# Seven Strassen units at the front of four up groups, with more room for their sums, in a one-layer hybrid decoder kernel

## The chip, the core and the metric

The kernel runs as one program on one core of a Trainium2 chip. The core's engines work from queues of their own and wait for each other by semaphores: PE multiplies matrices, DVE (VectorE) and ACT (ScalarE) do elementwise work, POOL (GpSimd) and SP issue DMAs. The metric is the device time of one execution, in microseconds (us); the time given is the median of several runs.

## What is computed

The reference computes one layer in float32 on 256 rows of 2048 channels:

```python
h = x
a = rmsnorm(h, attn_norm);  proj = a @ w_in          # two attentions follow, 16 heads
h = h + concat(out_mla, out_moba) @ w_o
f = rmsnorm(h, ffn_norm)
h = h + (silu(f @ w_gate) * (f @ w_up)) @ w_down     # w_gate, w_up: 2048 x 5632; w_down: 5632 x 2048
g = sigmoid(rmsnorm(h, ple_norm) @ w_ple_gate)
h = h + g * (p @ w_ple_proj);  out = rmsnorm(h, final_norm)
```

The change concerns the third part, the SwiGLU network, and there the four later products with w_up.

## The kernel before

**Three products for one.** A float32 product is made of float32r matmuls. Each operand is split into a high part, the operand rounded to float32r, and a low part, the rest. `three` (L350 to L352) issues the high activation by the high weight, the low activation by the high weight, and the high activation by the low weight. The high part of a weight is made by ACT (`split_hi`, L329, a CAST), the low part by DVE (`split_lo`, L337, raw minus high), which therefore waits for ACT.

**Groups, units, jobs.** A group is one product of the 256 rows with 1024 weight columns, accumulated in four PSUM banks (two row tiles by two column halves). It has units of two 128-row slices of the weight (1 MB of float32, one DMA into one of five raw buffers). A plain unit takes 2 slices x 2 halves x 2 row tiles x 3 = 24 matmuls of 128x512. The order of the groups in the SwiGLU network is g0, u0, then for c = 1 to 4: gate gc, the first half of the down product of the block before (dc0), up uc, the second half (dc1); then gu5 and the last down products. Gate and up groups have 8 units, down groups 4.

**Strassen units.** Some units of gate and up groups go by Strassen's scheme (in Winograd's form): the two slices by the two column halves are a 2x2 matrix of weight blocks, the two slices by the two row tiles one of activation blocks, and seven block products stand in for eight. `seven` (L392 on) issues them in four turns of 6, 3, 6 and 6 matmuls, 21 in all, into seven banks: three are the group's own, four others hold m1, m7, m5 and m6. In the run of such units of a group these four banks are taken from the rotating ones. After the last unit of the run ACT copies m1 to a tile U and DVE adds the other three in four instructions (L415 to L419). U is added to the group's banks when the group ends (L380 for an up group, by a DMA for a gate group).

The weights of such a unit cost more to prepare. `plan` gives it four jobs in place of two: the blocks "11 22" (1024 columns per partition), "21" (512), and the sums "t1 t3" and "t4 t2" (1024 each). Each job has a high part by ACT and a low part by DVE, and DVE makes the sums in three instructions (L340 with 1024 elements, L341 and L342 with 512), from raw, in place. A plain unit has two jobs of 1024. In down groups one job of 2048 does for the unit.

**The ring.** The parts lie in a ring of places of 512 columns: 12 in the ring proper, 4 in `more`, and 4 in `most`. A job takes 2 places (4 for a down unit's, 1 for "21"), and a job that would lie across the end of one of the three tiles begins at the next. `plan` notes for each job the last turn that reads the places it takes. The loop at the kernel's end puts a job's instructions in the queues of ACT and DVE ahead of turn j only if all turns that read its places are before j. So what ACT and DVE do is in the order of the jobs, and how far ahead of PE they are is bounded by the ring. Into the same queues go, at their place in the program, the evacuations: the four copies of a down group's banks at its end (`add_later`, L862, ACT, then a DMA by POOL that adds them to `hd` in DRAM), the silu (L969, ACT, two instructions, four steps after the gate group), the up group's end (L380 and L978, DVE), and the transposes of the block (`ff_transpose`: PE L1000, then ACT L121 and DVE L122, during the next gate group).

**Which units.** `mixed` names the eight units of a gate or up group in their order; S marks a Strassen unit. Before, the four later up groups and the gates from g2 on have '6 S0 S1 S2 S3 S4 S5 7': plain, six Strassen, plain. g0 has none, u0 two, g1 five.

**The activations' sums.** The scheme needs four sums of activation blocks per Strassen unit, split in high and low. `act_transpose` makes them when the activations are normed, during wo1 and g0 (L155 to L159). Before, three of the four get tiles of their own (`sums`, `sums4`, `sums5h`, `sums5l`); the fourth is kept in float32 (`s4`) and split later, by `fourth_sums`, into a quarter of aT that the plain units no longer read.

## Time and profile before

| | us |
|---|---|
| runs: median (lowest to highest) | 1192.59 (1191.95 to 1192.99), three runs |
| the profiled execution, span from first to last instruction | 1190.6 |
| PE busy with matmuls | 1179.3 (99%) |
| PE weight loads busy | 984.3 (83%) |
| DVE busy | 916.9 (77%) |
| ACT busy | 699.5 (59%) |
| POOL busy | 42.4 (4%) |

The profile gives no time of its execution beside the span; the span lies 2.0 us below the median of the runs. One period of the SwiGLU network (u, d1, next g, next d0) takes 124.8 us in it, and there are four. Times below are counted from the start of the span. Up group u2 begins on PE at 661.4, the down group d21 at 701.0, g3 at 722.7, d30 at 764.4 and u3 at 786.2. In a view in order of time, a row has the start in us, the duration in us, engine, line and operation, what is written from what, the count of merged instructions, and in brackets the idle time of the engine just before, with what ended it. PE rows last 0.39 us, but the matmuls overlap: the distance between two starts is what counts.

### The profile page before, as it was taken

What the parts mean: (1) busy time and instruction counts of PE and PEld (TensorE: products, weight loads), DVE (VectorE), ACT (ScalarE), POOL (GpSimd) and SP (SyncE); (2) the same over time, 40 slices, a digit from 0 to 9 for tenths busy, and PEclk for the clock granted to TensorE, in tenths of its full rate; (3) what the DMA queues carried; (4) which work ended last, traced back from release to release, by engine and by line L of the source; (5) the groups of instructions that cost most, each with busy time, mean ns of one, the idle gap of its engine ahead of it and who ended that gap; (6) DMA issues with size and microseconds to landing.
All of it is one profiled execution on the core that took longest, in us unless ns stands there. A gap on an engine that the chain in (4) does not pass through costs nothing.

```text
span 1190.6 us, 14471 instructions
## 1 busy us (share of the span) xinstructions
PE 1179.3 (99%) x5501; PEld 984.3 (83%) x5501; DVE 916.9 (77%) x1082; ACT 699.5 (59%) x898; POOL 42.4 (4%) x56
## 2 busy tenths in 40 slices
PE   9999999999999999999999999999999999999996
PEld 7888888899888888888888888888888888888886
DVE  5654635656457668998999899989998999897474
ACT  6735655456556755465656565757475656465453
POOL 5200000000000000000000000000000000000000
PEclk9999999999999999999999999999999999999998
DMA  9654654435653867395867777786869586836631
GB/s 305 213 190 122 214 168 151 150 111 199 247 210 112 315 222 273 107 308 167 297 182 258 231 240 225 221 274 207 252 217 276 193 256 212 339 138 219 210 106 71
DMA packets 79734, 250.30 MB, mean 210 GB/s; under 512 B 4844, under 2 KB 9248, under 8 KB 78384
## 3 DMA queue, kind: packets, MB, share of 16 engines
q1 hardware_dynamic: 75744, 229.93, 54.2%
q0 software_dynamic: 3632, 18.93, 8.8%
q8 instruction: 43, 0.70, 0.2%
q10 hardware_dynamic: 288, 0.52, 0.1%
q14 instruction: 27, 0.22, 0.1%
HBM read 228.39 MB, written 12.58 MB: 202 GB/s over the span
## 4 chain that ended last, share of the span: by engine, by line
PE 85%; DVE 9%; ACT 3%; issue 2%; DVEq 0%; ACTq 0%; POOL 0%; POOLq 0%
PE bank L352 27%; PE bank L350 27%; PE bank L351 27%; DVE ringl L337 3%; ACT ringh L329 1%; DVE raw L340 1%; PE bank L138 1%; DVE most L337 1%; PE bank L541 1%; DVE raw L341 1%; PE bank L662 1%; DVE raw L342 1%; PE bank L1000 1%; PE bank L570 0%; PE bank L544 0%
## 5 line engine op out<-in xcount | busy, mean ns | idle before, releaser
L337 DVE TENSOR_TENSOR ringl<-raw,ringh 128x1024 fp32r<-128x1024 f32 (+4 forms) x298 | 433.7, 1484 | 130.0 <-ACT ringh L329 124.1
L329 ACT CAST ringh<-raw 128x1024 fp32r<-128x1024 f32 (+4 forms) x298 | 366.0, 1263 | 283.7 <-PE bank L351 137.0
L350 PE MATMUL bank<-ringh,aT 128*128 128x512 f32 (+3 forms) x780 | 301.4, 386 | 0.0
L352 PE MATMUL bank<-ringl,aT 128*128 128x512 f32 (+3 forms) x780 | 296.8, 380 | 0.1
L351 PE MATMUL bank<-ringh,aT 128*128 128x512 f32 (+3 forms) x780 | 296.2, 380 | 0.0
L352 PEld LDWEIGHTS bank<-ringl,aT 128*128 128x128 f32 x780 | 146.5, 188 | 28.5 <-DVE ringl L337 1.5
L351 PEld LDWEIGHTS bank<-ringh,aT 128*128 128x128 f32 x780 | 146.8, 188 | 26.0
L350 PEld LDWEIGHTS bank<-ringh,aT 128*128 128x128 f32 x780 | 146.8, 188 | 26.0 <-ACT aT L124 0.3
L329 ACT CAST moreh<-raw 128x1024 fp32r<-128x1024 f32 (+2 forms) x68 | 79.1, 1192 | 45.2 <-DVE raw L340 36.0
L337 DVE TENSOR_TENSOR morel<-raw,moreh 128x1024 fp32r<-128x1024 f32 (+2 forms) x64 | 83.5, 1329 | 0.9 <-ACT moreh L329 0.2
L350 PE MATMUL bank<-ringh,ffTh 128*128 128x512 f32 x204 | 79.4, 389 | 0.0
L351 PE MATMUL bank<-ringh,ffTl 128*128 128x512 f32 x204 | 79.4, 389 | 0.0
L352 PE MATMUL bank<-ringl,ffTh 128*128 128x512 f32 x204 | 79.4, 389 | 0.0
L329 ACT CAST most<-raw 128x1024 fp32r<-128x1024 f32 (+2 forms) x55 | 54.6, 1017 | 35.9 <-DVE raw L340 30.6
L340 DVE TENSOR_TENSOR raw<-raw 128x1024 f32<-128x1024 f32 x57 | 69.5, 1219 | 0.0
L337 DVE TENSOR_TENSOR most<-raw,most 128x1024 fp32r<-128x1024 f32 (+2 forms) x55 | 63.2, 1171 | 1.8 <-ACT most L329 1.5
L352 PEld LDWEIGHTS bank<-ringl,ffTh 128*128 128x128 f32 x204 | 38.3, 188 | 8.0
L351 PEld LDWEIGHTS bank<-ringh,ffTl 128*128 128x128 f32 x204 | 38.3, 188 | 7.9
L350 PEld LDWEIGHTS bank<-ringh,ffTh 128*128 128x128 f32 x204 | 38.3, 188 | 7.9
L342 DVE TENSOR_TENSOR raw<-raw 128x512 f32<-128x512 f32 x57 | 39.5, 692 | 1.9
L341 DVE TENSOR_TENSOR raw<-raw 128x512 f32<-128x512 f32 x57 | 39.5, 692 | 1.9
L352 PE MATMUL bank<-most,aT 128*128 128x512 f32 x94 | 37.0, 394 | 0.0
(334 smaller groups left out, 1804.5 us busy)
## 6 DMA issues: line engine op xcount, KB each, us to landing
raw<-in_w_down SPq DMA_DIRECT2D x44, 1024.0 KB, 4.9
raw<-in_w_gate SPq DMA_DIRECT2D x40, 1024.0 KB, 7.0
raw<-in_w_up SPq DMA_DIRECT2D x40, 1024.0 KB, 8.3
raw<-in_w_in SPq DMA_DIRECT2D x40, 512.0 KB, 4.5
raw<-in_w_o SPq DMA_DIRECT2D x16, 1024.0 KB, 5.0
raw<-in_w_ple_gate SPq DMA_DIRECT2D x16, 1024.0 KB, 4.9
raw<-in_w_in SPq DMA_DIRECT2D x8, 1024.0 KB, 5.0
hd<-copied POOLq DMA_DIRECT2D x8, 1024.0 KB, 9.4
```

Of the source, the lines that this page charges most:

```text
L138: nc.tensor.transpose(b[:, (2 * i + t) * 128:(2 * i + t + 1) * 128], part[:, t, i * 128:(i + 1) * 128], ident)
L329: nc.scalar.copy(h[:, :, c0:c1], r[:, :, c0:c1])
L337: tt(l[:, :, c0:c1], r[:, :, c0:c1], h[:, :, c0:c1].bitcast(F32), op=ALU.subtract)
L340: tt(f[:, 0:2], f[:, 1:2].to_broadcast([128, 2, 512]), f[:, 0:4:3], op=ALU.subtract)
L341: tt(f[:, 3], f[:, 3], f[:, 0], op=ALU.subtract)
L342: tt(f[:, 2], f[:, 2], f[:, 3], op=ALU.subtract)
L350: nc.tensor.matmul(b, xh, h, start=start, stop=False)
L351: nc.tensor.matmul(b, xl, h, start=False, stop=False)
L352: nc.tensor.matmul(b, xh, l, start=False, stop=stop)
L541: nc.tensor.matmul(s[:, c0:c0 + nk], qT[:, q * 128:(q + 1) * 128], kT[:, 0:nk], start=True, stop=qpe is None)
L662: nc.tensor.transpose(b[:, (2 * i + t) * 128:(2 * i + t + 1) * 128], src[:, t, col(i0 + i):col(i0 + i) + 128], ident)
L1000: nc.tensor.transpose(b[:, (2 * i + t) * 128:(2 * i + t + 1) * 128], st[:, t, (k + i) * 128:(k + i + 1) * 128], ident)
```

## The change

1. `SEVENS` is 7 in place of 6, so that unit 6 has its activation sums too.
2. `mixed` gives the up groups u1 to u4 the order 'S0 S1 S2 S3 S4 S5 S6 7': seven Strassen units from the group's start, then one plain unit. The gate groups keep theirs.
3. All four sums of a unit are made and split at once in `act_transpose` (one split of 512 elements in place of 384), and `fourth_sums` with its calls is gone. The sums lie in `att`, a new tile `more_sums` (12 KB per partition), `tabs` and `ra`.
4. The room is taken from the scratch for the descriptors of DMAs that POOL issues: `dynamic_dma_scratch_size` is set to 4096 bytes per partition, where it was left at its default of 16384.
5. In `split_lo` the first sum of the weight blocks is issued ahead of the low part of "21" in place of behind it. This holds for all Strassen units. In the new numbering the low parts are L340 and the sums L339, L342 and L343.

```diff
@@ act_transpose
-        some = some.rearrange("q a (b c) -> q (a b) c", b=2)[:, 0:3]
+        four = some.rearrange("q a (b c) -> q (a b) c", b=2)
         tt = nc.vector.tensor_tensor
-        tt(some[:, 0], a21, a22, op=ALU.add)
-        tt(some[:, 1], some[:, 0], a11, op=ALU.subtract)
-        tt(some[:, 2], a21, a11, op=ALU.subtract)
-        tt(sums[2], a12, some[:, 1], op=ALU.subtract)
-        split_psum(sums[0], sums[1], some)
+        tt(four[:, 0], a21, a22, op=ALU.add)
+        tt(four[:, 2], a21, a11, op=ALU.subtract)
+        tt(four[:, 1], four[:, 0], a11, op=ALU.subtract)
+        tt(four[:, 3], a12, four[:, 1], op=ALU.subtract)
+        split_psum(sums[0], sums[1], four)
@@ split_lo
+        f = quarters(jb) if jb.kind == "21" else None
+        if f is not None:
+            tt(f[:, 0:2], f[:, 1:2].to_broadcast([128, 2, 512]), f[:, 0:4:3], op=ALU.subtract)
         tt(l[:, :, c0:c1], r[:, :, c0:c1], h[:, :, c0:c1].bitcast(F32), op=ALU.subtract)
-        if jb.kind == "21":
-            f = quarters(jb)
-            tt(f[:, 0:2], f[:, 1:2].to_broadcast([128, 2, 512]), f[:, 0:4:3], op=ALU.subtract)
+        if f is not None:
             tt(f[:, 3], f[:, 3], f[:, 0], op=ALU.subtract)
             tt(f[:, 2], f[:, 2], f[:, 3], op=ALU.subtract)
@@
-    SEVENS = 6
+    SEVENS = 7
@@ ffn_norm_half
-                    S["sums"] = big.tile([128, 2, 4, 3, 128], F32R, name="sums", tag="att")
...
+                    sums = [big.tile([128, 2, 3, 4, 128], F32R, name=f"sums{x}", tag=x) for x in ("att", "more_sums")]
+                    last = [big.tile([128, 4, 128], F32R, name="sums6h", tag="tabs"),
+                            work.tile([128, 4, 128], F32R, name="sums6l", tag="ra", bufs=1)]
+                    S["sums"] = [[x[:, i, n] for x in sums for n in range(3)] + [last[i]] for i in range(2)]
@@ gate_evac, gate_add, up_evac: the calls of fourth_sums go, and with them
-    def fourth_sums(*pairs):
-        for n in pairs:
-            split_psum(*(aT[i][:, 2 * n, 128:256] for i in range(2)), S["s4"][n])
@@ mixed
-        pairs = {'g0': '0 1 2 3 4 5 6 7', 'u0': '6 7 S0 S1 2 3 4 5', 'g1': '6 5 S0 S1 S2 S3 S4 7'}.get(name, '6 S0 S1 S2 S3 S4 S5 7').split()
+        pairs = {'g0': '0 1 2 3 4 5 6 7', 'u0': '6 7 S0 S1 2 3 4 5', 'g1': '6 5 S0 S1 S2 S3 S4 7'}.get(
+            name, '6 S0 S1 S2 S3 S4 S5 7' if name[0] == 'g' else 'S0 S1 S2 S3 S4 S5 S6 7').split()
@@
-    nc = bacc.Bacc("TRN2", target_bir_lowering=False, num_devices=1)
+    nc = bacc.Bacc("TRN2", target_bir_lowering=False, num_devices=1, dynamic_dma_scratch_size=4096)
```

What this does to the queues is shown at three places. In the rows, `raw_N` is the raw buffer of a unit, so the rows of one unit share it; ringh and ringl, moreh and morel, most are the high and low parts in the ring's three tiles.

**DVE, from the last unit of d20 to the front of u2.** Before: the job of d20's last unit (2048), unit 6 in two jobs, then S0 and the first of S1.

```order
L337 TENSOR_TENSOR ringl<-raw_113,ringh 128x2048
L337 TENSOR_TENSOR ringl<-raw_114,ringh 128x1024 x2
L337 TENSOR_TENSOR ringl<-raw_2796,ringh 128x1024
L337 TENSOR_TENSOR ringl<-raw_2796,ringh 128x512
L340 TENSOR_TENSOR raw_2796<-raw_2796 128x1024
L341 TENSOR_TENSOR raw_2796<-raw_2796 128x512
L342 TENSOR_TENSOR raw_2796<-raw_2796 128x512
L337 TENSOR_TENSOR morel<-raw_2796,moreh 128x1024 x2
L337 TENSOR_TENSOR most<-raw_2831,most 128x1024
L337 TENSOR_TENSOR most<-raw_2831,most 128x512
L340 TENSOR_TENSOR raw_2831<-raw_2831 128x1024
```

Now:

```order
L340 TENSOR_TENSOR morel<-raw_113,moreh 128x2048
L340 TENSOR_TENSOR most<-raw_114,most 128x1024
L339 TENSOR_TENSOR raw_114<-raw_114 128x1024
L340 TENSOR_TENSOR most<-raw_114,most 128x512
L342 TENSOR_TENSOR raw_114<-raw_114 128x512
L343 TENSOR_TENSOR raw_114<-raw_114 128x512
L340 TENSOR_TENSOR ringl<-raw_114,ringh 128x1024 x2
L340 TENSOR_TENSOR ringl<-raw_2796,ringh 128x1024
L339 TENSOR_TENSOR raw_2796<-raw_2796 128x1024
L340 TENSOR_TENSOR ringl<-raw_2796,ringh 128x512
L342 TENSOR_TENSOR raw_2796<-raw_2796 128x512
L343 TENSOR_TENSOR raw_2796<-raw_2796 128x512
```

S0 (raw_114) now follows d20's last unit directly, and S1 (raw_2796) follows S0; the first sum of a unit stands ahead of the low part of its "21".

**ACT, across the four copies at the end of d20** (L862 before, L863 now). Before:

```order
L329 CAST moreh<-raw_2796 128x1024 x2
L329 CAST most<-raw_2831 128x1024
L329 CAST most<-raw_2831 128x512
L862 COPY copied<-bank_77 128x512
L862 COPY copied<-bank_78 128x512
L862 COPY copied<-bank_79 128x512
L862 COPY copied<-bank_80 128x512
L329 CAST ringh<-raw_2831 128x1024 x2
L969 ACTIVATE stage<-stage,rf 128x1024 x2
L329 CAST ringh<-raw_112 128x1024
```

Now:

```order
L329 CAST ringh<-raw_2796 128x1024
L329 CAST ringh<-raw_2796 128x512
L329 CAST ringh<-raw_2796 128x1024 x2
L863 COPY copied<-bank_77 128x512
L863 COPY copied<-bank_78 128x512
L863 COPY copied<-bank_79 128x512
L863 COPY copied<-bank_80 128x512
L329 CAST moreh<-raw_2828 128x1024
L329 CAST moreh<-raw_2828 128x512
L951 ACTIVATE stage<-stage,rf 128x1024 x2
L329 CAST most<-raw_2828 128x1024 x2
```

Before, the copies stood within S1 (raw_2831), and the silu between S1 and S2. Now they stand between S1 (raw_2796) and S2 (raw_2828), and the silu within S2.

**DVE at the front of g3, around the four instructions on the transposed block** (L122). Before:

```order
L337 TENSOR_TENSOR ringl<-raw_113,ringh 128x1024
L337 TENSOR_TENSOR ringl<-raw_113,ringh 128x512
L340 TENSOR_TENSOR raw_113<-raw_113 128x1024
L341 TENSOR_TENSOR raw_113<-raw_113 128x512
L342 TENSOR_TENSOR raw_113<-raw_113 128x512
L337 TENSOR_TENSOR ringl<-raw_113,ringh 128x1024
L122 TENSOR_TENSOR ffTl<-bank_77,ffTh 128x512
L122 TENSOR_TENSOR ffTl<-bank_78,ffTh 128x512
L122 TENSOR_TENSOR ffTl<-bank_79,ffTh 128x512
L122 TENSOR_TENSOR ffTl<-bank_80,ffTh 128x512
L337 TENSOR_TENSOR morel<-raw_113,moreh 128x1024
L337 TENSOR_TENSOR morel<-raw_114,moreh 128x1024
```

Now:

```order
L340 TENSOR_TENSOR ringl<-raw_113,ringh 128x1024
L339 TENSOR_TENSOR raw_113<-raw_113 128x1024
L340 TENSOR_TENSOR ringl<-raw_113,ringh 128x512
L342 TENSOR_TENSOR raw_113<-raw_113 128x512
L343 TENSOR_TENSOR raw_113<-raw_113 128x512
L122 TENSOR_TENSOR ffTl<-bank_77,ffTh 128x512
L122 TENSOR_TENSOR ffTl<-bank_78,ffTh 128x512
L122 TENSOR_TENSOR ffTl<-bank_79,ffTh 128x512
L122 TENSOR_TENSOR ffTl<-bank_80,ffTh 128x512
L340 TENSOR_TENSOR ringl<-raw_113,ringh 128x1024 x2
L340 TENSOR_TENSOR morel<-raw_114,moreh 128x1024
```

The jobs lie at other places of the ring, and "t1 t3" of S1 (the sixth row before) has moved behind the transposed block, to its fellow "t4 t2". It is so in g2 and g3; in g4 and gu5 the order is as before.

More of the change, by code (lines that the diff above doesn't have):

```diff
@@ L900, in scale @@
                         nc.scalar.mul(S["nrm"][:, (k // 2) % 2, t], S["h"][:, t, k * 128:k * 128 + 256], S["rs"][:, t:t + 1])
-                if k0:
-                    s4 = work.tile([128, 2, 128], F32, name="s4c", tag="junk")
-                    S["s4"] += [s4[:, i] for i in range(2)]
-                    S["sums"][0].append(work.tile([128, 3, 128], F32R, name="sums5h", tag="ra", bufs=1))
-                    S["sums"][1].append(big.tile([128, 3, 128], F32R, name="sums5l", tag="mask"))
                 scale(k0)
@@ L912, in g @@
                 for k in range(k0, k0 + 8, 2):
-                    sums = [*(S["sums"][i][k // 2] for i in range(2)), S["s4"][k // 2]] if k // 2 < SEVENS else None
+                    sums = [S["sums"][i][k // 2] for i in range(2)] if k // 2 < SEVENS else None
                     act_transpose(S["h"], k, G_FFN, aT, scaled=True, sums=sums)
@@ L980, in f @@
             if left["n"] == 0:
-                if ci == 0:
-                    fourth_sums(*(2, 3, 4))
                 turned = ff_transpose(ci, n, S.pop("ff"))
```

11 lines of the change are left out of this document (removed).

## The prediction

> **What bounds the kernel now.** I read the page's busy times, then the busy times of one period of the SwiGLU network, then the chain of waits there, then PE and DVE in order of time.
>
> ```profile
> PE 1179.3 (99%) x5501; PEld 984.3 (83%) x5501; DVE 916.9 (77%) x1082; ACT 699.5 (59%) x898; POOL 42.4 (4%) x56
> ```
>
> ```profile
> 661.40:786.20 124.80, 124.75 (x558) 102.80 (x557) 117.24 (x119) 77.79 (x85) 3.92 (x4) 1.00 0.74 236
> ```
>
> Over the span PE looks like the only bound. In the period (second row: length, then busy PE, weight loads, DVE, ACT, POOL, granted clock) DVE is busy 117.24 of 124.8 us, 94%. The chain of waits of the same period runs more through DVE than through any line of PE:
>
> ```profile
> by line: DVE ringl L337 14.3%; PE bank L352 12.9%; PE bank L351 12.6%; PE bank L350 12.6%; issue 10.3%; DVE raw L340 7.3%; ACT ringh L329 5.7%; DVE raw L341 3.9%; DVE most L337 3.8%; DVE raw L342 3.1%; DVE U L380 1.9%; DVE stage L978 1.8%;
> ```
>
> Now PE in u2, first its front (start of the plain unit 6, start of S0), then the second half of its last unit's first bank, then a place in g3:
>
> ```profile
> 661.38 0.39 PE L350 MATMUL bank<-ringh,aT 128*128 128x512 f32 x1
> ...
> 666.82 0.39 PE L350 MATMUL bank<-ringh,aT 128*128 128x512 f32 x1
> ```
>
> ```profile
> 696.53 0.49 PE L352 MATMUL bank<-most,aT 128*128 128x512 f32 x1
> 696.87 0.40 PE L350 MATMUL bank<-moreh,aT 128*128 128x512 f32 x1
> ```
>
> ```profile
> 755.99 0.39 PE L351 MATMUL bank<-ringh,sums5l 128*128 128x512 f32 x1
> 756.43 0.50 PE L352 MATMUL bank<-ringl,sums5h 128*128 128x512 f32 x1
> ```
>
> 24 matmuls take 666.82 - 661.38 = 5.44 us, 0.227 each. A Strassen unit's 21 take 4.76. Two starts that lie further apart are a wait: 0.34 after the last low part of u2's weights (0.1 lost), and 0.44 within S5 of g3 (0.2 lost). Apart from steps of 0.1 where transposes stand between, these are the waits of the period, and both are for low parts (L352), that is for DVE. So PE never stops for long, but DVE is just in time at the end of both runs. Here is DVE from the last unit of d20 to the end of u2's jobs:
>
> ```profile
> 644.59 6.29 DVE L337 TENSOR_TENSOR ringl<-raw,ringh 128x2048 fp32r<-128x2048 f32 x5
> ...
> 656.37 1.83 DVE L337 TENSOR_TENSOR most<-raw,most 128x1024 fp32r<-128x1024 f32 x2 [0.49 <-ACT most L329]
> ...
> 663.15 2.36 DVE L337 TENSOR_TENSOR ringl<-raw,ringh 128x1024 fp32r<-128x1024 f32 x2 [2.37 <-ACT ringh L329]
> 667.12 1.83 DVE L337 TENSOR_TENSOR ringl<-raw,ringh 128x1024 fp32r<-128x1024 f32 x2 [1.61 <-ACT ringh L329]
> 668.87 1.22 DVE L340 TENSOR_TENSOR raw<-raw 128x1024 f32<-128x1024 f32 x1
> 670.12 0.69 DVE L341 TENSOR_TENSOR raw<-raw 128x512 f32<-128x512 f32 x1
> ...
> 675.61 1.22 DVE L340 TENSOR_TENSOR raw<-raw 128x1024 f32<-128x1024 f32 x1
> ...
> 695.26 1.22 DVE L337 TENSOR_TENSOR most<-raw,most 128x1024 fp32r<-128x1024 f32 x1
> 696.68 2.29 DVE L337 TENSOR_TENSOR ringl<-raw,ringh 128x2048 fp32r<-128x2048 f32 x1 [0.21 <-ACT ringh L329]
> ```
>
> From one unit's L340 to the next, 668.87 to 675.61, a Strassen unit takes DVE **6.74 us**, against 4.76 on PE. Within the run DVE falls behind by 2 us per unit and lives off its lead, which the ring bounds. From 667.12 (S2's first job) four units and the last unit's two jobs of 1.22 make 667.12 + 4 x 6.74 + 2.44 = 696.5; the last one does end at 695.26 + 1.22 = 696.48. So the run is DVE without a gap. DVE's idle time lies ahead of it: 0.49 + 2.37 + 1.61 = 4.47 us, all for ACT's high parts.
>
> **Part 1: fewer matmuls.** Four groups lose 3 matmuls each: 12 x 0.227 = 2.7 us of PE, 0.68 per group. This is a gain only where PE need not wait.
>
> **Part 2: DVE's work in an up group.** Unit 6 cost two jobs, 2.44 us; as a Strassen unit it costs 6.74: 4.30 us more per group. What of that fits into the 4.47 us of idle time is decided by the ring, at the group's front. I follow u2. DVE ends d20's last job at 644.59 + 2.29 = 646.9 (the first of the row's five; its length as in the row at 696.68) and has S0 and S1 ready 2 x 6.74 later, at 660.4. S2's first job takes places of the ring that d20's last unit holds (in all four groups); PE is done with that unit at 661.38, and ahead of S2's cast in ACT's queue now stand all four copies of d20's banks. The last copy waits for the same end of PE:
>
> ```profile
> 661.58 0.59 ACT L862 COPY copied<-bank 128x512 f32<-128x512 f32 x1 [0.77 <-PE bank L352]
> 662.07 2.00 ACT L329 CAST ringh<-raw 128x1024 fp32r<-128x1024 f32 x2
> 663.96 2.19 ACT L969 ACTIVATE stage<-stage,rf 128x1024 f32<-128x1024 f32 x2
> ```
>
> So the cast behind the copies starts at 662.07, as before, and DVE's next job at 663.15, as before; only that this job was S1's "t1 t3" and is now the first of S2. The idle time there is 663.15 - 660.4 = 2.8 us and cannot be filled: nothing else is in the queue. The silu's 2.19 us, which cost the idle 1.61, now lies between S2's "21" and its sums on ACT. A cast of 1024 takes 1.0, one of 512 about 0.6 (half a cast and the fixed rest; an estimate from the 2.00 of two), so ACT has S2's "t1 t3" at 663.1 + 0.6 + 2.19 + 1.05 = 666.9, and DVE asks for it 6.74 - 2.42 later than 663.15, at 667.5. Covered, by half a microsecond; with that cover gone up to 1.6 comes back per group.
>
> From 663.15 DVE has S2 to S6 and the last unit: 663.15 + 5 x 6.74 + 2.44 = 699.3, against 696.5 by the same sum before: **2.77 us later**. PE alone would be there earlier: 661.38 + 7 x 4.76 + 5 matmuls = 695.8. It waits 3.5 us, in S5, S6 and at the last unit's second job, and everything behind is 2.77 us later than before: the last unit, U's use, d's first products. DVE itself is as much later as PE, so the next gate group meets the same lead as before. Four groups: **11.1 us**.
>
> **Part 3: the gates' fronts.** The other ring places put both sum jobs of S1 behind the transposed block's four instructions in g2 and g3.
>
> ```profile
> 724.80 1.22 DVE L337 TENSOR_TENSOR ringl<-raw,ringh 128x1024 fp32r<-128x1024 f32 x1
> 727.03 2.48 DVE L122 TENSOR_TENSOR ffTl<-bank,ffTh 128x512 fp32r<-128x512 f32 x4 [1.01 <-ACT ffTh L121]
> 729.44 2.36 DVE L337 TENSOR_TENSOR morel<-raw,moreh 128x1024 fp32r<-128x1024 f32 x2
> ```
>
> ```profile
> 724.47 2.04 ACT L862 COPY copied<-bank 128x512 f32<-128x512 f32 x4
> 726.38 2.09 ACT L121 CAST ffTh<-bank 128x512 fp32r<-128x512 f32 x4
> ```
>
> ```profile
> 725.44 1.91 PE L1000 MATMUL bank<-ident,stage 128*128 128x128 f32 x16
> ```
>
> DVE now comes to L122 without the 1.22 us of "t1 t3" (row at 724.80). The copies are no longer held by that job's cast, so the first ffTh starts with the first four transposes, 725.44 + 1.91/4 = 725.9, not 726.38, and DVE starts L122 at about 726.5. It ends at 729.0, but S1's "t1 t3" has its cast only behind the four ffTh (725.9 + 2.09 + 1.05 = 729.05), two jobs take 2.4, and S2 starts at 731.4; before, at 729.44 + 1.18 = 730.6. 0.8 us, and g's run is just in time (the wait at 756.43): **1.6 us** in two groups. Bounds: 0 if the run's order makes it up, 1.22 each if ffTh comes no earlier.
>
> **Part 4: the moved sum.** Ahead or behind, it is the same instruction. An instruction that waits for the one before starts 1.25 after a 1.22 (668.87, 670.12); one that doesn't overlaps it: 668.87 - 667.12 = 1.75 for 1.22 + 0.69, 0.08 each. So a wait costs 0.11. Before, two instructions of a unit had such a wait (L341, L342); now again two (L339, which overwrites what the low part of "11 22" reads, and L343). I take 0. Bounds: 0.11 per unit either way, on five units of each up group and six of each of four gates: 44 x 0.11 = 4.8 us.
>
> **Part 5: sums and scratch.**
>
> ```profile
> L122 DVE TENSOR_TENSOR aT<-s4vb,aT x2: 285/288/292, 431.9 to 432.1; 128x128 fp32r<-128x128 f32 x2
> ...
> 396.57 0.69 DVE L122 TENSOR_TENSOR aT<-stage,aT 128x512 fp32r<-128x512 f32 x1 [4.84 <-ACT aT L121]
> ```
>
> Six late splits of 0.29 go, and a seventh unit's sums (four of 0.3, a split of 0.69) come in g0, where DVE had just idled 4.84: nothing on the path; uncovered it would be some 2 us either way. The smaller scratch matters to POOL's DMAs:
>
> ```profile
> 641.64 0.86 POOL L965 DMA_DIRECT2D stage<-U  x1 [38.55 <-ACT stage L961]
> 662.46 1.08 POOL L865 DMA_DIRECT2D hd<-copied  x1 [19.96 <-ACT copied L862]
> ```
>
> One is issued at a time, 20 us apart; if a transfer had to be issued in pieces, the silu at 663.96 still lies 22 us behind its DMA. I take 0.
>
> **Sum:** 1190.6 (span) + 11.1 + 1.6 = 1203.3. The runs' median lies 2.0 above the span of the profiled execution: **1205.3 us**, of its own between 1201 and 1209 (part 4's 4.8 either way is the largest bound).
>
> **Rivals.** *PE alone decides* (faster). If DVE kept ahead, the 12 matmuls would be the whole effect: 1192.6 - 2.7 = 1189.9. It decides if u's last low part comes by 695.8, so if a Strassen unit takes (695.8 - 663.15 - 2.44) / 5 = 6.05 us or less. For it: the 99%; and the moved sum lets ACT start "t1 t3" earlier. Against: between 668.87 and 675.61 DVE has no gap that an earlier cast could close, and six instructions of these lengths don't shrink. 6%. [...]
>
> *The idle time is filled* (no change). If S2 could start when S1 is done, at 660.4, u's last job would end at 660.4 + 33.7 + 2.44 = 696.5, as before: 1192.6 + 1.6 = 1194.2. For it: 4.47 us idle and 4.30 more work. Against: the ring and the copies. 8%.
>
> *More is lost at the front* (slower). If the silu's cover fails, 1.61 more per group: 1205.3 + 6.4 = 1211.7. For it: a margin of half a microsecond worked out from four casts. 10%.
>
> *The change does not do what it says*: the scratch holds POOL's DMAs up beyond their lead of 22 us, or the run at the front stalls on banks (m6's, copied by 661.58 + 0.59 = 662.2, is asked for 15 matmuls after 661.38, at 664.8). 2%, mostly slower.
>
> **Numbers.** My forecast has 74%. The range reaches up to the third rival and leaves out the first two and the forecast's edges, some 18% together: 1200 to 1212. A measurement of this kernel can tell about 0.2% (2.4 us) from no change. Faster 6% (first rival); same 7% (second); slower 87%.
>
> **What would show it.** In the profile after: PE starts in u2's S5 and S6 lie 1 to 2 us apart at their third turn (t1 t3), about 3.5 us per group in all, none in S0 to S3; the up group takes 42.3 us in place of 39.5 (two plain and six Strassen units and 0.1); DVE idles some 2.8 us ahead of S2, and not behind it; a Strassen unit takes DVE 6.74; g2 and g3 are 0.8 longer, g4 is not. I am wrong if PE's starts in the up groups stay 0.227 apart, or if DVE's S2 starts before PE has left the down group.

## The result and the profile after

| | before | with the change |
|---|---|---|
| median of the runs, us | 1192.55 (1191.95 to 1192.99) | **1204.87** (1204.56 to 1205.29) |
| ratio to before | | **1.0103**, 95% interval 1.0091 to 1.0115 |
| span of the profiled execution, us | 1190.6 | 1202.8 |
| PE busy, matmul records | 1179.3, 5501 | 1180.2, 5489 |
| DVE busy | 916.9 | 934.5 |

The kernel is 1.0% slower, by 12.3 us; the prediction was 1205.3. First the busy times of the page, then the period from u2 to the start of u3 (columns as in the prediction's row for this period), then the chain of waits in it.

```profile
PE 1180.2 (98%) x5489; PEld 980.9 (82%) x5489; DVE 934.5 (78%) x1100; ACT 706.9 (59%) x902; POOL 42.4 (4%) x56
```

```profile
665.11:793.50 128.39, 125.16 (x555) 101.97 (x553) 121.49 (x124) 79.42 (x87) 3.92 (x4) 1.00 0.73 230
```

```profile
by line: PE bank L353 21.5%; PE bank L351 20.5%; PE bank L352 20.5%; issue 10.4%; DVE ringl L340 7.6%; DVE morel L340 3.4%; DVE raw L342 3.3%; DVE raw L343 2.8%; DVE most L340 2.1%; DVE ffTl L122 1.7%; ACT moreh L329 1.7%; ACT ringh L329 1.
```

Twelve matmuls fewer, and PE takes longer: it now has unfilled time inside the period, 128.39 - 125.16 = 3.2 us, where it had 0.05. DVE has 4.25 us more work in a period that is 3.6 us longer. The chain's shares mislead here: more of them go to PE than before, because the chain crosses to DVE only at the few places where PE stands. Those places are seen in PE's own rows. In u2 the two longest are the third turn of S5 and S6:

```profile
692.73 0.50 PE L353 MATMUL bank<-most,sumsmore_sums 128*128 128x512 f32 x1 [1.14 <-DVE most L340]
...
697.89 0.39 PE L352 MATMUL bank<-ringh,sums6l 128*128 128x512 f32 x1
699.46 0.50 PE L353 MATMUL bank<-ringl,sums6h 128*128 128x512 f32 x1 [1.18 <-DVE ringl L340]
```

The releaser in brackets is each time DVE's low part of "t1 t3". And DVE, from the last job of S1 to the end of u2's jobs:

```profile
661.58 2.48 DVE L340 TENSOR_TENSOR ringl<-raw,ringh 128x1024 fp32r<-128x1024 f32 x2
666.88 1.23 DVE L340 TENSOR_TENSOR morel<-raw,moreh 128x1024 fp32r<-128x1024 f32 x1 [2.82 <-ACT moreh L329]
668.14 1.22 DVE L339 TENSOR_TENSOR raw<-raw 128x1024 f32<-128x1024 f32 x1
...
674.88 1.22 DVE L339 TENSOR_TENSOR raw<-raw 128x1024 f32<-128x1024 f32 x1
...
701.74 1.22 DVE L340 TENSOR_TENSOR morel<-raw,moreh 128x1024 fp32r<-128x1024 f32 x1
```

2.82 us idle ahead of S2, 6.74 us from one unit's L339 to the next (668.14, 674.88), and no gap until the group's last job has ended at 703.0. What DVE waits for ahead of S2 is seen on ACT: the cast of S2's "11 22" stands behind the last of the four copies, and the silu behind that cast.

```profile
665.31 0.59 ACT L863 COPY copied<-bank 128x512 f32<-128x512 f32 x1 [0.77 <-PE bank L353]
665.79 1.57 ACT L329 CAST moreh<-raw 128x1024 fp32r<-128x1024 f32 x2
667.26 2.19 ACT L951 ACTIVATE stage<-stage,rf 128x1024 f32<-128x1024 f32 x2
669.47 1.05 ACT L329 CAST most<-raw 128x1024 fp32r<-128x1024 f32 x1
```

The last of these rows makes S2's "t1 t3" ready at 670.52; DVE's low part for it starts at 671.21, so the silu is covered by 0.7 us. DVE in g3, from the transposed block to S2's first job:

```profile
733.19 2.48 DVE L122 TENSOR_TENSOR ffTl<-bank,ffTh 128x512 fp32r<-128x512 f32 x4 [1.82 <-ACT ffTh L121]
735.60 2.36 DVE L340 TENSOR_TENSOR ringl<-raw,ringh 128x1024 fp32r<-128x1024 f32 x2
737.88 1.22 DVE L340 TENSOR_TENSOR morel<-raw,moreh 128x1024 fp32r<-128x1024 f32 x1
```

S1's two sum jobs (the second row) stand behind the block, as the prediction's third part has it.

Where the 12.2 us of the span lie is best seen in the lengths of the groups, each taken from its first matmul to that of the next group. All other groups and stages stay within 0.1 us, the start (to g0) within 0.2.

| us | u1 | u2 | u3 | u4 | g2 | g3 | g4 | gu5 |
|---|---|---|---|---|---|---|---|---|
| before | 39.57 | 39.57 | 39.57 | 39.59 | 41.71 | 41.71 | 41.72 | 41.69 |
| with the change | 42.38 | 42.34 | 42.34 | 42.34 | 42.79 | 42.53 | 41.40 | 41.38 |
| difference | +2.81 | +2.77 | +2.77 | +2.75 | +1.08 | +0.82 | -0.32 | -0.31 |

Up groups +11.1, g2 and g3 +1.9, g4 and gu5 -0.6. The last two had not been foreseen.

### The profile page after: what moved, and what is told of

It is laid out like the page before. It is cut to its first block, busy times and chain, and to the rows that moved or that the text cites. A ratio compares the mean times of both kernels' runs of the same rounds, so it can differ in the third digit from the quotient of the medians.

```text
span 1202.8 us, 14488 instructions
## 1 busy us (share of the span) xinstructions
PE 1180.2 (98%) x5489; PEld 980.9 (82%) x5489; DVE 934.5 (78%) x1100; ACT 706.9 (59%) x902; POOL 42.4 (4%) x56
## 3 DMA queue, kind: packets, MB, share of 16 engines
q1 hardware_dynamic: 75744, 229.93, 54.2%
## 4 chain that ended last, share of the span: by engine, by line
PE 89%; DVE 6%; issue 2%; ACT 2%; ACTq 0%; POOL 0%; DVEq 0%; POOLq 0%
PE bank L353 28%; PE bank L351 28%; PE bank L352 28%; DVE ringl L340 2%; PE bank L138 1%; DVE raw L342 1%; ACT ringh L329 1%; DVE raw L343 1%; PE bank L542 1%; PE bank L980 1%; DVE morel L340 1%; PE bank L663 1%; DVE raw L339 1%; DVE most L340 0%; PE bank L571 0%
## 5 line engine op out<-in xcount | busy, mean ns | idle before, releaser
L340 DVE TENSOR_TENSOR ringl<-raw,ringh 128x1024 fp32r<-128x1024 f32 (+4 forms) x299 | 435.3, 1474 | 122.2 <-ACT ringh L329 117.6
L351 PE MATMUL bank<-ringh,aT 128*128 128x512 f32 (+3 forms) x730 | 281.9, 386 | 0.0
L353 PE MATMUL bank<-ringl,aT 128*128 128x512 f32 (+3 forms) x730 | 277.9, 381 | 0.0
L352 PE MATMUL bank<-ringh,aT 128*128 128x512 f32 (+3 forms) x730 | 276.7, 379 | 0.0
L353 PEld LDWEIGHTS bank<-ringl,aT 128*128 128x128 f32 x730 | 137.1, 188 | 27.5 <-DVE ringl L340 2.6
L352 PEld LDWEIGHTS bank<-ringh,aT 128*128 128x128 f32 x730 | 137.3, 188 | 24.0
L351 PEld LDWEIGHTS bank<-ringh,aT 128*128 128x128 f32 x730 | 137.4, 188 | 23.9 <-ACT aT L124 0.3
L340 DVE TENSOR_TENSOR morel<-raw,moreh 128x1024 fp32r<-128x1024 f32 (+2 forms) x68 | 88.9, 1322 | 3.7 <-ACT moreh L329 3.0
L329 ACT CAST most<-raw 128x1024 fp32r<-128x1024 f32 (+2 forms) x58 | 58.1, 1022 | 38.1 <-DVE raw L339 23.2
L352 PE MATMUL bank<-ringh,ffTl 128*128 128x512 f32 x204 | 79.4, 389 | 0.0
L339 DVE TENSOR_TENSOR raw<-raw 128x1024 f32<-128x1024 f32 x61 | 74.7, 1225 | 2.0
L340 DVE TENSOR_TENSOR most<-raw,most 128x1024 fp32r<-128x1024 f32 (+2 forms) x58 | 68.2, 1182 | 0.6 <-ACT most L329 0.2
L352 PEld LDWEIGHTS bank<-ringh,ffTl 128*128 128x128 f32 x204 | 38.3, 188 | 7.9
L343 DVE TENSOR_TENSOR raw<-raw 128x512 f32<-128x512 f32 x61 | 42.2, 692 | 2.1
L342 DVE TENSOR_TENSOR raw<-raw 128x512 f32<-128x512 f32 x61 | 41.8, 684 | 0.0
L351 PE MATMUL bank<-moreh,aT 128*128 128x512 f32 x87 | 34.1, 392 | 0.0
```

The lines of the kernel that those rows point to most:

```text
L329: nc.scalar.copy(h[:, :, c0:c1], r[:, :, c0:c1])
L339: tt(f[:, 0:2], f[:, 1:2].to_broadcast([128, 2, 512]), f[:, 0:4:3], op=ALU.subtract)
L340: tt(l[:, :, c0:c1], r[:, :, c0:c1], h[:, :, c0:c1].bitcast(F32), op=ALU.subtract)
L342: tt(f[:, 3], f[:, 3], f[:, 0], op=ALU.subtract)
L343: tt(f[:, 2], f[:, 2], f[:, 3], op=ALU.subtract)
L351: nc.tensor.matmul(b, xh, h, start=start, stop=False)
```

## Experiments

My theory: the up group's loss is DVE's work on the five Strassen units S2 to S6, counted from the moment S2 may start: more than DVE's lead over PE can bear. Rivals: the place at the group's front, the moved sum, the sums' room or the smaller scratch, and PE.

### All of the change but the order of the up groups

```diff
-            name, '6 S0 S1 S2 S3 S4 S5 7' if name[0] == 'g' else 'S0 S1 S2 S3 S4 S5 S6 7').split()
+            name, '6 S0 S1 S2 S3 S4 S5 7' if name[0] == 'g' else '6 S0 S1 S2 S3 S4 S5 7').split()
```

> The change with the order of the up groups as before (6 S0 S1 S2 S3 S4 S5 7): what is left is the moved sum, the activation sums in other room, and the smaller scratch. My theory as corrected by the trace (the moved sum lets ACT cast t1 t3 earlier, and what stands behind it in ACT's queue): up groups 39.57 as before, the four later gates 0.3 shorter each or unchanged, 1191.5, within 1190.5 to 1192.6. The prediction had 0 for all of this: 1192.5. Rival, the sums, the scratch or the moved sum carry a part of the loss: above 1193.5.

1191.24 us, 0.9989 of before (0.9980 to 0.9999). Up groups 39.57, the four later gates 41.35 to 41.37, which is 0.35 less each; 4 x 0.35 = 1.4 us, which is all of the 1.3 us gained in the median. The stretch from g0 to g1's end, where the activation sums are now made in other room, takes 129.57 as before (129.59). So the sums and the scratch cost nothing that these times show, and the whole loss is in the order.

### The moved sum put back

```diff
-        if f is not None:
-            tt(f[:, 0:2], f[:, 1:2].to_broadcast([128, 2, 512]), f[:, 0:4:3], op=ALU.subtract)
         tt(l[:, :, c0:c1], r[:, :, c0:c1], h[:, :, c0:c1].bitcast(F32), op=ALU.subtract)
         if f is not None:
+            tt(f[:, 0:2], f[:, 1:2].to_broadcast([128, 2, 512]), f[:, 0:4:3], op=ALU.subtract)
```

> The change with the double sum put back behind the low part of the quarter 21. If the moved sum is what made g4 and gu5 0.3 us shorter than before, they go back to 41.7, g2 and g3 get longer by up to as much, up groups stay at 42.3: 1205.5 to 1206.2. If the order of these two instructions is worth nothing (the prediction): 1204.9, with g4 and gu5 still at 41.4. Rival, the moved sum costs a wait per Strassen unit (0.11 each): below 1204 and a Strassen unit's 6.74 on DVE at 6.6.

1205.72 us, 1.0112 (1.0097 to 1.0127); the interval overlaps that of the change, so the times alone don't separate the two. The groups do: g4 and gu5 are back at 41.73 and 41.70, g2 and g3 stay at 42.77 and 42.50. ACT at the front of g4, with the change and then with the sum put back (the first sum is L339 in the one and L340 in the other):

```profile
857.93 1.05 ACT L329 CAST ringh<-raw 128x1024 fp32r<-128x1024 f32 x1 [2.28 <-DVE raw L339]
858.89 2.04 ACT L863 COPY copied<-bank 128x512 f32<-128x512 f32 x4
860.96 2.06 ACT L121 CAST ffTh<-bank 128x512 fp32r<-128x512 f32 x4
```

```profile
858.84 1.06 ACT L329 CAST ringh<-raw 128x1024 fp32r<-128x1024 f32 x1 [2.76 <-DVE raw L340]
859.79 2.04 ACT L862 COPY copied<-bank 128x512 f32<-128x512 f32 x4
861.70 1.60 ACT L121 CAST ffTh<-bank 128x512 fp32r<-128x512 f32 x3
```

g4 starts at 857.60 and at 858.04. The cast of S1's "t1 t3" waits for the first sum. With the sum ahead it starts 0.33 after the group in place of 0.80, and the casts of the transposed block, behind it and the copies in ACT's queue, start 3.36 after the group in place of 3.66: the 0.3 us of the group. In g2 and g3 this cast stands behind the block, so nothing there depends on it. That also says why a "free" exchange of two instructions on DVE was worth something: it costs DVE nothing (a unit of u2 takes it 6.74 us either way), but ACT waits for one of them.

### Six units at the front: the place alone

```diff
-            name, '6 S0 S1 S2 S3 S4 S5 7' if name[0] == 'g' else 'S0 S1 S2 S3 S4 S5 S6 7').split()
+            name, '6 S0 S1 S2 S3 S4 S5 7' if name[0] == 'g' else 'S0 S1 S2 S3 S4 S5 6 7').split()
```

> The change with six Strassen units at the front of u1 to u4 and units 6 and 7 plain behind them: the position alone, with as many matmuls and as much DVE work as before. My theory (S2 cannot start before 663.15 on DVE, from there 6.74 per unit): S2 to S5 end at 663.15 + 4 x 6.74 = 690.1, PE alone would be through them at 661.38 + 6 x 4.76 = 689.9; so PE waits once, in S5's third turn, some 1.3 us, and no more, since the two plain units take DVE 4.88 and PE 10.88. Up group 40.8 to 40.9 us (39.57 before, 42.34 with seven); u's four groups +5.2. With the gates as they are in the change (g2, g3 +0.9 each or 0, g4 and gu5 -0.3): 1197.5, within 1196.5 to 1200. Rival, the loss is the seventh unit's DVE work alone: up group 39.57, 1192.5. Rival, the loss is all from the place at the front: up group 42.3, 1204.9.

1201.38 us, 1.0076 (1.0061 to 1.0091): above my range. The up groups are as expected, 40.91 to 40.94, and PE waits once, in S5's third turn:

```profile
691.98 0.50 PE L353 MATMUL bank<-morel,sumsmore_sums 128*128 128x512 f32 x1 [1.14 <-DVE morel L340]
```

So with the same matmuls and the same DVE work as before, the place alone costs 1.35 us per group: the plain unit 6 in front had given DVE 5.44 us of PE's time for 2.44 of its own. The seventh unit costs the other 1.4. The miss lies in the gates. All four take 42.47 to 42.53, since this order leaves the ring so that S1's "t1 t3" stands behind the transposed block in all four; that is 4 x 0.8 = 3.2 us where I had allowed 1.2 at most. The 0.8 us of the prediction's third part are thus not a matter of seven units but of where a group leaves the ring.

### The price of a unit on DVE: one sum less, two sums less

```diff
             tt(f[:, 3], f[:, 3], f[:, 0], op=ALU.subtract)
-            tt(f[:, 2], f[:, 2], f[:, 3], op=ALU.subtract)
+            if units[jb.unit].name not in ("u1", "u2", "u3", "u4"):
+                tt(f[:, 2], f[:, 2], f[:, 3], op=ALU.subtract)
```

> The change without the second sum of 128x512 (L343) in the Strassen units of u1 to u4; these groups then use one quarter of the weights as an unfinished sum, so the output is another. A unit takes DVE 6.74 - 0.69 to 0.72 = 6.02 to 6.05 us, level with the 6.05 from which, by the prediction's sum, PE alone sets the up group. My theory (the length of the up group is DVE's from S2 to the last unit, 5 units at this price, and PE's 38.76 where that is more): 42.34 - 5 x 0.7 = 38.8, so 38.8 to 39.0, and 1190.5 to 1191.5, where leaving out both sums gave 38.76 and 1190.5. Rival, what counted in that run was the chain through ACT's cast of t4 t2, which both sums delay: about half way, 40.5, 1197.5.

The other kernel leaves both sums out in these groups:

> The change without the two sums of 0.69 us (raw from raw, 128x512) in the Strassen units of u1 to u4; these groups then use two quarters of the weights as they are, so the output is another. A unit takes DVE some 5.3 us in place of 6.74, below the 6.05 worked out in the prediction's first rival. My theory (DVE's work is the loss): no waits of PE in the runs of the up groups, up group 7 x 4.76 + 5.44 + 0.1 = 38.9 us, 42.3 with the change; four groups 13.8 us less, and g2, g3 at most 1 us each less: 1191, within 1189 to 1192. Rival, the wait is for the ring, for banks or for the casts at the group's front: up group above 41, above 1199.

1190.73 us (0.9983, 0.9973 to 0.9993) with one sum less and 1190.53 (0.9983, 0.9974 to 0.9992) with two. u2's DVE with one sum less, from S2 on:

```profile
664.62 1.23 DVE L340 TENSOR_TENSOR morel<-raw,moreh 128x1024 fp32r<-128x1024 f32 x1 [4.28 <-ACT moreh L329]
665.88 1.23 DVE L339 TENSOR_TENSOR raw<-raw 128x1024 f32<-128x1024 f32 x1
...
671.89 1.23 DVE L339 TENSOR_TENSOR raw<-raw 128x1024 f32<-128x1024 f32 x1
```

and u2 as a window (length, PE busy, weight loads, DVE, and so on), with one sum less and with two:

```profile
662.85:701.68 38.83, 38.83 (x173) 32.08 (x171) 36.55 (x37) 28.67 (x30) 1.08 (x1) 1.00 0.68 208
```

```profile
661.53:700.29 38.76, 38.76 (x172) 32.09 (x171) 33.83 (x33) 28.31 (x30) 1.08 (x1) 1.00 0.67 209
```

0.72 us less per unit (6.02 in place of 6.74) shortens the group by 3.5, nearly five times as much. A second sum less (5.93, since DVE now waits 0.59 per unit for a cast) gives nothing more, as 7 x 4.76 + 5.44 = 38.76 is PE's own time. This is in keeping with the point from which PE decides, worked out in the first rival as 6.05 us per unit: at 6.02 the group is 0.07 above PE's time, at 6.74 it is 3.6 above. Between the two nothing was run. DVE still idles 4.28 us ahead of S2 with one sum less, more than with the change, and it does no harm: the idle time is not the loss. The change itself shows the same: DVE idles 4.04 us ahead of S2 in u1 and 2.82 in u2, S2 starts 1.77 after the group in both, and the groups last 42.38 and 42.34.

### More room in the ring

```diff
-    RING = 12
+    RING = 13
...
-    nc = bacc.Bacc("TRN2", target_bir_lowering=False, num_devices=1, dynamic_dma_scratch_size=4096)
+    nc = bacc.Bacc("TRN2", target_bir_lowering=False, num_devices=1, dynamic_dma_scratch_size=1024)
```

> The change with 13 places in the ring in place of 12 (the room from a scratch of 1024 bytes). S2's first job then takes places that d20's third unit holds, not its last, and is issued ahead of d20's last matmuls; S2's three other jobs stay behind. The gates' S1 gets its t1 t3 ahead of the transposed block in all four groups, as g4 has it in the change. My theory: DVE does one job of 1.22 in the idle time ahead of S2 (2.82 in the change, 1.6 here), and each up group is 1.2 shorter, 41.1; g2 and g3 at 41.4 in place of 42.79 and 42.53: 1204.9 - 4.9 - 2.5 = 1197.5, within 1196 to 1199. Rival, DVE's work alone sets the up group and its front does not matter: 42.3, and 1202.4. Rival, the gates' 0.8 to 1.1 comes from the up groups' delay and not from S1's place: g2, g3 stay at 42.5.

1195.62 us, 1.0028 (1.0017 to 1.0039). The gates are at 41.35, all four, and the up groups at 40.48, shorter than I had expected:

```profile
660.59 2.36 DVE L340 TENSOR_TENSOR most<-raw,most 128x1024 fp32r<-128x1024 f32 x2
662.98 1.22 DVE L339 TENSOR_TENSOR raw<-raw 128x1024 f32<-128x1024 f32 x1
...
667.21 3.50 DVE L340 TENSOR_TENSOR ringl<-raw,ringh 128x1024 fp32r<-128x1024 f32 x3 [1.00 <-ACT ringh L329]
```

Not only S2's "11 22" went into the idle time but also its first sum (L339), which needs no place in the ring; 1.82 of the 2.82 us are filled, and the group is 1.86 shorter. The 1.00 that is left is a wait for the cast of S2's "t1 t3", which starts at 666.15, behind the silu. The stretch from g0 to g1's end got 1.0 us longer, to 130.61, by one wait of PE in g1 that ends with DVE's part of the transposed block (L122):

```profile
489.04 0.50 PE L351 MATMUL bank<-ringh,sumsatt 128*128 128x512 f32 x1 [0.71 <-DVE ffTl L122]
```

The next kernel, with the scratch of 4096 bytes, waits at the same place (1.87 us in its row), which speaks for the other ring places and against the smaller scratch.

With three places more, for which some activation sums share their room:

```diff
-                    sums = [big.tile([128, 2, 3, 4, 128], F32R, name=f"sums{x}", tag=x) for x in ("att", "more_sums")]
+                    sums = [big.tile([128, 2, 3, 4, 128], F32R, name="sumsatt", tag="att")] * 2
...
-    RING = 12
+    RING = 15
```

> The change with 15 places in the ring, for which the activation sums of units 3 to 5 lie in the room of those of units 0 to 2 (so the later units overwrite the earlier ones' sums, and the output is another; instructions and their sizes stay). S2's 11 22, its quarter 21 and its sums, 4.3 us of DVE, are issued ahead of d20's last matmuls. My theory: the idle time ahead of S2 is filled, DVE runs from S0 to the last unit without a gap, the up group takes 39.6 as before the change, the gates 41.4: 1204.9 - 11.1 - 2.5 = 1191.3, within 1190 to 1193. That is the prediction's second rival made real. Rival, the idle time turns up elsewhere in the group (behind S2, for casts that stand behind the copies and the silu): up group above 40.5, above 1195.

1201.83 us, 1.0081 (1.0066 to 1.0096), far from my 1191.3. Three things make up most of the 10.5 us: 3.3 in the up groups, 3.3 in the gates, and 3.1 ahead of g1's end (132.68 from g0, 2 of it the wait just named). u1 takes 39.56, as expected; u2 to u4 take 40.66 to 40.74: DVE runs through S2 now, but stops ahead of S3, whose cast stands behind the silu on ACT. DVE, then ACT, in u2 (which starts at 666.32):

```profile
673.16 1.23 DVE L340 TENSOR_TENSOR ringl<-raw,ringh 128x1024 fp32r<-128x1024 f32 x1 [1.80 <-ACT ringh L329]
```

```profile
670.00 2.19 ACT L951 ACTIVATE stage<-stage,rf 128x1024 f32<-128x1024 f32 x2
672.09 1.55 ACT L329 CAST ringh<-raw 128x1024 fp32r<-128x1024 f32 x2
```

So the rival named in the expectation holds for three groups of four, and it is the mechanism of the prediction's third rival, with the silu one unit later. The gates g2 to g4 are at 42.48 to 42.54, gu5 at 41.37. Here S1 is complete ahead of the transposed block in those three, and that is too much of it: the copies then stand behind the cast of its "t4 t2", and PE's transposes, which need the copied banks, wait for them (ACT, then PE, in g3, which starts at 728.74):

```profile
731.00 1.05 ACT L329 CAST most<-raw 128x1024 fp32r<-128x1024 f32 x1 [0.86 <-DVE raw L343]
731.95 2.04 ACT L863 COPY copied<-bank 128x512 f32<-128x512 f32 x4
```

```profile
732.58 1.63 PE L980 MATMUL bank<-ident,stage 128*128 128x128 f32 x12 [0.96 <-ACT copied L863]
```

Over all kernels with the moved sum a gate is shortest, 41.35 to 41.5, where S1's "t1 t3" is ahead of the block and its "t4 t2" behind it. It is 1.1 to 1.4 longer where both are behind, and 1.1 to 1.2 where both are ahead.

**One sum for all of these.** Take the time after the group's start at which DVE begins to run without a gap (t), add the work that it has left then, and add a constant for what PE does after the last low part. The constant, 4.43, is set by the change's own u2, whose units S2 to S6 and two jobs make 36.14; the other rows are then free, though their t is read from their own traces: this is an account of where the time lies, and no forecast. (With 13 places S3's first job starts at 670.74 - 1.26 = 669.48, as a unit's L339 starts 1.26 behind it, so 2.27 us from 667.21.)

| u group | t, us | DVE's work left | sum + 4.43 | measured |
|---|---|---|---|---|
| with the change, u2 | 666.88 - 665.11 = 1.77 | 5 x 6.74 + 2.44 = 36.14 | (42.34) | 42.34 |
| before, u2 | 667.12 - 661.38 = 5.74 | 4 x 6.74 + 2.44 = 29.40 | 39.57 | 39.57 |
| 13 places, u2 | 667.21 - 662.85 = 4.36 | 2.27 of S2 + 29.40 = 31.67 | 40.46 | 40.48 |
| 15 places, u2 | 673.16 - 666.32 = 6.84 | 29.40 | 40.67 | 40.66 |
| 15 places, u1 | 546.50 - 540.76 = 5.74 | 29.40 | 39.57 | 39.56 |
| one sum less, u2 | 1.77 | 5 x 6.02 + 2.44 = 32.54 | 38.74 (PE: 38.76) | 38.83 |

Four groups of three kernels come out within 0.02 us. The last row is 0.1 off and no test, since PE's own time is as long there. Where DVE's work is the bound, what sets an up group is not how long DVE idles ahead of a unit, but when after the group's start it last has to stand, and what it has left to do then.

### Moving the sums to POOL

```diff
         if f is not None:
+            if units[jb.unit].name in ("u1", "u2", "u3", "u4"):
+                tt = nc.gpsimd.tensor_tensor
             tt(f[:, 3], f[:, 3], f[:, 0], op=ALU.subtract)
             tt(f[:, 2], f[:, 2], f[:, 3], op=ALU.subtract)
```

> The change with the two sums of 128x512 (L342, L343) of the Strassen units of u1 to u4 on POOL in place of DVE; the output is the reference's. A unit then takes DVE 5.4 to 5.9 us, below the 6.05 from which PE would set the up group. What one such sum takes on POOL no row here shows; the nearest is 0.91 for 128x128 (L497), so between 0.9 (if none of it grows with size) and 3.6 (if all does). My theory at up to about 2.2 per sum: no waits of PE in the runs, up group 38.8, 1190.5, as without these sums. At 3.6, 7.2 per unit, POOL is the bound: 663 + 5 x 7.2, up group above 44, above 1210. Rival, the up group does not hang on DVE: 42.3 whatever POOL takes.

With only the second of them (L343) on POOL:

> The change with only the second of these sums (L343) on POOL in u1 to u4; the output is the reference's. A unit takes DVE 6.74 - 0.69 = 6.05 us and a little, which is just the 6.05 at which the prediction's sum has PE and DVE level. My theory at up to 2 us on POOL: up group 38.8 to 39.3, 1190.5 to 1192.5. At 3.6 on POOL the cast of t4 t2 comes 2.9 later and DVE, which has 1.2 of other work there, idles 1.7 in each unit: up group above 42. Rival, the up group's length does not follow DVE's time per unit in proportion: above 40.5 though POOL is fast.

1255.47 us, 1.0533 (1.0517 to 1.0549), and 1243.91, 1.0432 (1.0417 to 1.0448): both expectations failed, though POOL's rows are about as long as I had allowed (1.61 us for the first sum, 2.15 for the second). The up groups take 52.8 to 54.2 and 50.7 to 52.1, and the down groups ahead of them are up to 2.2 and 1.4 longer. DVE with both on POOL:

```profile
699.60 2.36 DVE L340 TENSOR_TENSOR ringl<-raw,ringh 128x1024 fp32r<-128x1024 f32 x2 [2.26 <-ACT ringh L329]
...
708.30 2.36 DVE L340 TENSOR_TENSOR morel<-raw,moreh 128x1024 fp32r<-128x1024 f32 x2 [2.25 <-ACT moreh L329]
```

From the first row to the next of its kind a unit takes 8.70 us. I had counted DVE's work, not its order: the low part of "t4 t2" waits for ACT's cast, that for POOL, and DVE's next unit stands behind it. So I issued the "t4 t2" job of each unit behind the next unit's "11 22" and "21":

```diff
+    def slow(jb):
+        return jb.kind == "t4 t2" and units[jb.unit].name in ("u1", "u2", "u3", "u4")
...
+            slows = [x for x in todo if slow(x)]
+            todo = [x for x in todo if x not in slows]
+            at = next((k + 1 for k, x in enumerate(todo) if x.kind in ("21", "")), 0)
+            if at:
+                todo, held = todo[:at] + held + todo[at:], []
+            held += slows
+            if held and held[0].turn <= j:
+                todo, held = held + todo, []
...
+            done = min([done] + [x.unit - 1 for x in held])
```

> The change with both sums of 128x512 of the Strassen units of u1 to u4 on POOL, and the t4 t2 job of each such unit (cast and low part) issued behind the next unit's 11 22 and 21 jobs, so that DVE does 5.5 us of other work while POOL's 1.61 + 2.15 us and the cast's 1.05 run; the output is the reference's. My theory (POOL cost 53 us because DVE and ACT stood in their queues behind its sums, 2.25 idle per unit): a unit takes DVE 5.4 us and up to 0.4 where it runs beside POOL, 5.8, below 6.05; up group 38.8 to 39.2, the gates 41.4 to 42.7 as in the change; 1190.5 to 1193. Rival, POOL slows DVE down by sharing something, whatever the order: up group above 42, above 1203.

> The same with 13 places in the ring (scratch of 1024 bytes). By the runs so far 13 places bring all later gates to 41.35 and cost 1.0 us before g1's end. My theory: up groups 38.8 to 39.2 as in the run beside, 1195.6 - 4 x (40.48 - 38.8) = 1188.9, within 1188 to 1191. Rival, as beside: above 1197.

1229.11 us, 1.0307 (1.0291 to 1.0322), and 1219.46, 1.0223 (1.0208 to 1.0238). The waits for casts are gone and the group still takes 48 to 50 us (45.9 to 48.1 with 13 places). The rival was right. POOL and then DVE, with 12 places:

```profile
699.04 1.60 POOL L344 TENSOR_TENSOR raw<-raw 128x512 f32<-128x512 f32 x1 [3.61 <-issue]
700.72 2.15 POOL L345 TENSOR_TENSOR raw<-raw 128x512 f32<-128x512 f32 x1
```

```profile
699.42 2.29 DVE L340 TENSOR_TENSOR morel<-raw,moreh 128x1024 fp32r<-128x1024 f32 x1
701.64 2.30 DVE L340 TENSOR_TENSOR most<-raw,most 128x1024 fp32r<-128x1024 f32 x1
703.87 1.21 DVE L340 TENSOR_TENSOR ringl<-raw,ringh 128x1024 fp32r<-128x1024 f32 x1
```

A low part of this size takes DVE 1.21 to 1.23. Beside a sum of POOL's it takes 2.3, and it ends 1.07 after that sum, at 701.71 after 700.64 and at 703.94 after 702.87: it behaves as if it stood until POOL is done. Two sums moved away save DVE 1.4 us per unit and hold it up for 2.2; a unit takes it 7.44 us. It goes the other way too: POOL's second sum ends 1.16 behind the first of these low parts (702.87 after 701.71). In the kernel with only that sum on POOL no other sum stands ahead of it there, and it still takes 2.15, while the low part that started before it keeps its 1.22 (DVE, then POOL):

```profile
698.21 1.22 DVE L340 TENSOR_TENSOR ringl<-raw,ringh 128x1024 fp32r<-128x1024 f32 x1
```

```profile
698.43 2.15 POOL L345 TENSOR_TENSOR raw<-raw 128x512 f32<-128x512 f32 x1 [6.07 <-ACT ringh L329]
```

This sum ends at 700.58, 1.15 after that low part (699.43) though no other starts beside it, and the one above 1.16 after its low part though another does start beside it. By these rows whichever of the two is first is not held up by the other, and POOL's 1.61 and 2.15 us contain a wait for DVE.

### Strassen units where DVE has time

From the kernel with the old order in the up groups:

```diff
-        pairs = {'g0': '0 1 2 3 4 5 6 7', 'u0': '6 7 S0 S1 2 3 4 5', 'g1': '6 5 S0 S1 S2 S3 S4 7'}.get(
+        pairs = {'g0': '0 1 2 3 4 5 6 7', 'u0': '6 7 S0 S1 S2 S3 S4 5', 'g1': '6 5 S0 S1 S2 S3 S4 7'}.get(
```

> The change with the order of u1 to u4 as before (as in the run that had only that) and five Strassen units in u0 in place of two (6 7 S0 S1 S2 S3 S4 5): the change's room for the activation sums has all of them ready at the end of g0. In that run's u0 DVE idles 9.6 us between 426 and 451, and no down group's lead is needed since two plain units stand ahead. My theory (a Strassen unit pays 0.68 where DVE has the room): 3 x 0.68 = 2.0 less before g1's end (127.5 in place of 129.57), with at most one wait of a few tenths in S4; all later groups as in that run; 1191.2 - 2.0 = 1189.2, within 1188.5 to 1190. Rival, DVE's 12.9 us more use up the lead of g1, whose run follows without a down group between: waits of 1 us and more in g1, 1190.5 or above.

1199.48 us, 1.0060 (1.0048 to 1.0072). My theory fell, though not where I had looked. In u0's run PE waits a tenth twice. But DVE, with three units more, then has g1's jobs in its queue ahead of its use of u0's banks and U, comes to that 8.4 us later, and PE's transposes wait for the result: the rival's lack of lead, at another place. PE at the front of g1, and DVE's first instruction of that part:

```profile
481.81 0.48 PE L980 MATMUL bank<-ident,stage 128*128 128x128 f32 x1 [5.24 <-DVE stage L960]
484.58 1.75 PE L980 MATMUL bank<-ident,stage 128*128 128x128 f32 x7 [2.29 <-DVE stage L960]
```

```profile
480.29 0.68 DVE L381 TENSOR_TENSOR U<-U,bank 128x512 f32<-128x512 f32 x1
```

Without the three units the same instruction started at 471.90. The stretch from g0 to g1's end takes 137.80 in place of 129.57.

The fastest kernel with the reference's output is therefore the change without its new order, 1191.24 us: it beats the kernel before by 0.1%, at the edge of what can be told, and the change by 1.1%.

## Why the prediction was right

By its own steps, against u2 and g3 of the profile after; times are from the group's start.

| step | predicted | measured | |
|---|---|---|---|
| 1. 12 matmuls fewer are a gain only where PE need not wait | 0.68 saved per up group, outweighed by waits | 0.68 saved, 3.4 waited | right; 38.76 to 38.83 where DVE keeps up |
| 2. S2 blocked by ring and copies | idle 2.8, S2 at 1.77 | 2.82, S2 at 1.77 | right |
| 2. silu covered | no idle behind S2, cover 0.6 | none, cover 0.7 | right; with 13 and 15 places it uncovers |
| 2. a Strassen unit on DVE | 6.74 | 6.74 | right |
| 2. last job of u ends | 37.9 | 37.85 | right |
| 2. PE's waits in u2 | 3.5 in S5, S6, last unit | 3.4 in the same places, none earlier | right |
| 2. four groups | 11.1 | 11.1 | right |
| 3. g2, g3 | 0.8 each | 1.08, 0.82 | 1.9 in place of 1.6 |
| 3. L122 starts, S2 of g3 starts | 3.8, 8.7 | 3.98, 8.67 | right |
| 4. moved sum | 0 | -0.35 per gate where S1's "t1 t3" is ahead of the block | mis-sized |
| 5. sums and scratch | 0 | 0 (129.57 against 129.59) | right |
| sum, span | 1203.3 | 1202.8 | two misses partly cancel |

The four up groups, 11.1 of the 12.2 us, came out by the mechanism that the prediction gives. That the sum is as close as 0.5 us is in part luck: the gates g2 and g3 came out 0.3 longer together than forecast, and g4 and gu5 0.6 shorter.

The step that was off is the fourth. It asked what the exchange costs DVE, found nothing, and was right in that. It didn't ask who waits for the sum: ACT's cast of "t1 t3", with the copies and the transposed block's casts behind it. The first rival does say that the moved sum lets ACT start "t1 t3" earlier, but weighs it for the up groups alone. The two gates whose order the change leaves alone are 0.3 us shorter for it, 0.63 together, and putting the sum back undoes it. With the old order all four gates are 0.35 shorter, 1.4 together; that this too is the moved sum is inferred from its size, since the sum was not put back there. The bound given for it, 4.8 us either way, held that; its reason, a wait of 0.11 per unit, did not: with the sum put back a unit of u2 still takes DVE 6.74 us (its first sums start at 669.10 and 675.84).

Part 3's forecast is 0.28 us short in g2. DVE has one wait of 0.34 us there that g3 does not have, at 615.12, 11 us behind the transposed block, for a cast that itself waited for PE (L352) until 614.03. That this wait is the 0.28 was not tried.

Of the rivals, *PE alone decides* named its own condition, 6.05 us per unit, and the runs without sums show that it holds there and not at 6.74. *The idle time is filled* was made real in part: with one place more 1.86 of the 2.77 us come back, and with three all of them in u1 and 1.6 to 1.7 elsewhere. *More is lost at the front* did not happen with the change, but its mechanism, a cast behind the silu, is what stood in the way with 13 and 15 places. *The change does not do what it says* is out: the order is the whole loss.

The prediction read what bounds the kernel by span, where PE is busy 99%, and by period, where DVE is busy 94%. The runs decide for the period: relieving PE of 12 matmuls at the price of 4.25 us more of DVE's work per up group lost 12 us, and taking one instruction off DVE in the 28 units gained 14 against the change.

## What to carry to other kernels

Where two engines feed each other through a bounded ring, look for the last place at which the feeding engine must stand, and add up its work from there to the end of the run: that sum, not the share of busy time nor the idle time, told here whether a cheaper operation on the other engine was a gain (36.14 us of DVE's work from 1.77 after u2's start, against 29.40 from 5.74 before). A change that removes work from the engine that looks full and adds work to the one that feeds it has to pass that sum first. And when an instruction moves at no cost to its own engine, follow who waits for its result, since its gain or loss can appear in that queue, as the 0.3 us of g4 did on ACT.
